# Making the MLP's inner activations in pieces, and moving the first copies at a pass's end, in a GLA and squared-ReLU layer

## The chip, the cores and the metric

One core of a Trainium2 chip. Time is that of the device for one execution of the whole kernel, in microseconds; the median of three runs of the kernel before is 1090.81 us (1090.51 to 1090.86). A profile is one further execution, taken by the hardware profiler.

Names used below: PE is TensorE (PEld its weight loads), DVE is VectorE, ACT is ScalarE, POOL is GpSimd, SP is the engine that issues the loads.

## The reference

One layer on 256 tokens of width 2048, all in float32: a normalization, a chunked gated linear attention with its projections, a residual sum, then the part that the change touches:

```python
h = h + _sq_relu_mlp(_rmsnorm(h, mlp_norm), w_up, w_down)   # w_up 2048 x 8192, w_down 8192 x 2048
def _sq_relu_mlp(h, w_up, w_down):
    a = jax.nn.relu(h @ w_up)
    return (a * a) @ w_down
```

and a final normalization. The inner activations are `a * a`, 8192 values for each token.

## The kernel before

**Products.** Each float32 operand is split into a high part (ACT, a cast, `copy_hi`, line 114) and a low part (DVE, the operand minus its high part, lines 124 and 147). A product is three matmuls: high by high, high by low, low by high. High and low parts of weights lie in five slots each (tags `hi` and `lo`), which are taken in turn, so a part can be made only when PE is through with the part five places back.

**Up.** The MLP runs in eight rounds of 1024 inner columns. A round has two groups of 512, and a group has eight up steps (`turned_steps`, line 182), each with one load of 512 KB, one high part, one low part and 24 matmuls. A group's sums lie in two PSUM banks.

**Forms.** When a group ends, DVE applies the ReLU and the normalization (`normalized`, line 714, output `su`), ACT squares (line 723, into `work`), DVE makes three or so differences (line 727) and ACT and DVE split all forms into high and low parts (`act`, lines 734 and 735). A group has two halves, and both use one buffer in `work` for their forms, one after the other.

**Down.** A pass is one round's activations by one column group of 512 outputs (`g`, four of them); the passes of a round go through the groups forward in odd rounds and backward in even ones, so the last group of a round is the first of the next. A pass has four units (`kp` 0 to 3), each of 256 inner rows: a load, high and low part of it, products. Most units are *summed* units: a Strassen scheme with seven products of blocks. They use sums of blocks of the weights, which DVE makes into `work` (line 830), and which are split into parts in their turn (`of_sums`, line 845; in the trace `hi<-work`, `lo<-work`). The first unit of a pass is mostly *plain*: full products and no sums. Where a pass has the same group as the one before it, its first unit is summed too.

**Banks.** A pass accumulates in four PSUM banks, P16, B32, P57 and BX4. At a pass's end to another group each bank is copied to SBUF (`settle`, which runs `copy_end`, line 750) and a free bank is loaded with the next group's state (`begin`, also line 750). Both are ACT copies of 128x512 elements. A copy out of a bank waits until PE is through with the bank.

**Order.** Up steps run 18 steps ahead of the units (`LEAD`). A unit issues its load, its parts and its products, then one up step goes in (`next(steps)` after the unit's `yield`), then the unit's `of_sums`. The order on each engine is made by a planner that goes by the program's order and its own costs; `issue_after(x)` puts what is issued in its block behind x on x's engine. `copy_hi` stays behind the last copy of a bank, and `copy_end` behind the last high part and the last copy, so their order on ACT is the program's. In the kernel before, forms are issued in one go, right behind the first up step of the next group, behind that step's low part on DVE. P16's settle and begin are issued in the unit before the first summed unit, behind its up step (line 854); P57's in the first summed unit ahead of `of_sums` (line 857); those of B32 and BX4 for the next pass in the pass's last unit ahead of `of_sums` (line 860).

Of the kernel before, what the change touches and what calls it, by code (L numbers as in the profile page):

```python
# [28 lines left out]
F32R = mybir.dt.float32r  # L29
# [3 lines left out]
P = 128  # L33
# [35 lines left out]
def tile_gla_mlp(ctx, tc, x, xt, cols, w_vg, w_in, w_gate, w_out, w_up, w_down, final_norm, out):  # L69
# [33 lines left out]
    def flush():  # L103
        while side:
            side.popleft()()
# [10 lines left out]
    def slots():  # L116
        return [wpool.tile([P, SLOT], F32R, tag=i, name=i) for i in ("hi", "lo")]
# [549 lines left out]
    def by_sums(m, g, kp):  # L667

        if m == ROUNDS - 1:
            return (g, kp) in ((0, 0), (0, 2), (1, 2))  # L670
        if m == ROUNDS - 2 and g == order_of(m)[-1]:
            return kp in (1, 2)
        return kp > 0 or m > 0 and g == order_of(m)[0]
# [9 lines left out]
    free = deque([*firsts, *aux_free, *others])  # L683

    def up():
        ended = []
        for m in range(ROUNDS):
            for q in range(MR // GT):
                taken = [free.popleft() for _ in range(2)]
                acc = [psum_bank(i, "up") for i in taken]  # L690
                even = (6,) if m == q == 0 else (0,) if m == 0 else (3,) if q == 0 else ()
                for _ in turned_steps(lambda kt: (hth[:, kt], htl[:, kt]), w_up, m * MR + q * GT, even, acc, 1):

                    while ended:
                        with tc.issue_after(last_lo[0].ins):
                            ended.pop(0)()
                    yield
                if m == 0:
                    flush()

                def end(m=m, q=q, acc=acc, taken=taken):
                    act = big.tile([P, 4 * G + 64], F32R, tag="BC"[q], name="act")[:, OFF:-16]
                    acts[m][q] = act = act.rearrange("p (b i f s) -> p b i f s", b=2, i=2, f=8)
                    normal = [normalized(b) for b in acc]
                    for b in range(2):
                        forms(m, 2 * q + b, normal[b], act[:, b])
                    free.extend(taken)

                ended.append(end)
        ended.pop()()  # L710

    def normalized(bank):
        s = tmp.tile([P, 2, T], F32, tag="t512", name="su", bufs=3)
        nc.vector.scalar_tensor_tensor(
            s, bank.rearrange("p (i t) -> p i t", i=2), 0.0, r2row.unsqueeze(1).to_broadcast([P, 2, T]),
            op0=ALU.max, op1=ALU.mult,
        )
        return s

    def forms(m, kp, s, act):  # L720
        ways = {by_sums(m, g, kp) for g in range(GROUPS)}
        f = work[:, 2].rearrange("p (f s) -> p f s", f=8)
        nc.scalar.activation(
            f[:, A12:].rearrange("p (t i) s -> p i t s", t=2), s.rearrange("p i (t s) -> p i t s", t=2), AF.Square
        )
        if True in ways:
            sub = lambda o, x, y: nc.vector.tensor_tensor(o, x, y, op=ALU.subtract)  # L727
            sub(f[:, S3 : S1 + 1], f[:, A21:].to_broadcast([P, 2, P]), f[:, A11 : A22 + 1])
            sub(f[:, S2], f[:, A11], f[:, S1])
            sub(f[:, S4], f[:, A12], f[:, S2])  # L730
        some = slice(0 if True in ways else A12, 8 if False in ways else A21)
        x = f[:, some].rearrange("p f s -> p (f s)")
        oh, ol = (act[:, i, some].rearrange("p f s -> p (f s)") for i in range(2))
        nc.scalar.copy(oh, x)
        nc.vector.tensor_tensor(ol, x, oh.bitcast(F32), op=ALU.subtract)  # L735
# [53 lines left out]
    def down(passes):  # L789

        ahead = pending = None
        units = 0
        for n, (m, g) in enumerate(passes):
            fresh = not n or passes[n - 1][1] != g
            if fresh:
                banks = ahead or {k: begin(k, g) for k in (B32, BX4)}
                if m == ROUNDS - 1:  # L800
                    flush()
            ends = n + 1 == len(passes) or passes[n + 1][1] != g
            first = min(kp for kp in range(KP) if by_sums(m, g, kp)) if fresh else None
            for kp in range(KP):
                last = ends and kp == KP - 1
                by_parts = by_sums(m, g, kp)

                def product(k, o, a, w, c, banks=banks, last=last):

                    bank = banks[k][1]  # L810
                    for i, (x, y) in enumerate(((0, 0), (0, 1), (1, 0))):
                        halves(bank[:, o], a[x], w[y][:, c], bank.name not in used, last and i == 2)
                        used.add(bank.name)

                raw = raw_tile()[:, : 2 * GT]
                c0 = m * MR + 2 * kp * P
                src = w_down[c0 : c0 + 2 * P, g * GT : (g + 1) * GT].rearrange("(i p) c -> p i c", p=P)
                last_load[0] = nc.sync.dma_start(out=raw.rearrange("p (i c) -> p i c", i=2), in_=src)
                w = parts(raw, 2 * GT, slots(), [(T * by_parts, 2 * GT)])
                at = lambda f, m=m, kp=kp: stationary(m, kp, f)  # L820
                block = lambda i: slice(i * T, (i + 1) * T)
                if by_parts:
                    product(P16, left, at(A11), w, block(1))
                    product(B32, right, at(A12), w, block(3))
                    product(B32, left, at(S4), w, block(2))
                    wk = work[:, n_sums[0] % 2]
                    n_sums[0] += 1
                    u = wk.rearrange("p (f s) -> p f s", f=4)
                    raw = raw.rearrange("p (f s) -> p f s", f=4)
                    add = lambda o, x, y: nc.vector.tensor_tensor(o, x, y, op=ALU.add)  # L830

                    with tc.issue_after(last_lo[0].ins):
                        add(u[:, :2], raw[:, :1].to_broadcast([P, 2, T]), raw[:, 1:3])
                        add(u[:, 2], u[:, 0], raw[:, 2])
                        last_sum[0] = add(u[:, 3], u[:, 2], raw[:, 3]).ins
                else:
                    for i in range(2):
                        for k, f in ((B32, (A11, A12)), (BX4, (A21, A22))):
                            product(k, slice(0, GT), at(f[i]), w, slice(i * GT, (i + 1) * GT))
                if pending:  # L840
                    pending()
                    pending = None
                yield

                def of_sums(wk=wk if by_parts else None, product=product, at=at):

                    with tc.issue_after(last_lo[0].ins):
                        wu = parts(wk, G, slots())
                    product(P57, left, at(S1), wu, block(0))
                    product(P57, right, at(S3), wu, block(1))  # L850
                    product(P16, right, at(S2), wu, block(2))
                    product(BX4, right, at(A22), wu, block(3))

                if fresh and kp == first - 1:
                    settle(P16)
                    banks[P16] = begin(P16, g)
                if fresh and kp == first:
                    settle(P57)
                    banks[P57] = begin(P57, g)
                if last:  # L860
                    if n + 1 < len(passes):
                        ahead = {k: begin(k, passes[n + 1][1]) for k in (B32, BX4)}
                    else:
                        last_banks(0)
                if by_parts:
                    if units + LEAD < UPS:
                        of_sums()
                    else:

                        pending = of_sums  # L870
                units += 1
                if fresh and kp == first:
                    settle(B32, BX4)
            if ends:

                def end(k, i, bank, g=g):
                    copy_end(home(k, g), two(bank))
                    free.append(i)

                late.update({k: lambda k=k, end=end, of=banks[k]: end(k, *of) for k in range(4)})  # L880
                begun.add(g)
                if m == ROUNDS - 1 or m == ROUNDS - 2 and g > 1:
                    late[BX4] = lambda f=late[BX4], g=g: (f(), side.extend(combine(g)))
# [147 lines left out]
```

## Time and profile before

| | |
|---|---|
| median of the runs | 1090.81 us |
| the profiled execution | 1090.18 us |
| its span, first to last instruction | 1088.1 us |
| PE busy | 1074.5 us |
| DVE busy | 830.7 us |
| ACT busy | 678.0 us |
| mean granted TensorE clock | 0.997 |
| loaded from HBM | 206.92 MB |

The MLP's matmuls run from about 381 us to the end; a round is about 87 us. In a group of instructions the line stands first, then the engine, the operation, output<-inputs, shape and count; behind the bar the time busy, the mean of one in ns, and the time in which its engine stood idle just before it, with what ended that. In a list of waits stand the total, the number and the longest wait. In order of time stand the start, the time and, in brackets, the idle time before. A window shows each engine's busy time with the number of its instructions, the granted clock, and the share and the rate of DMA.

### The profile page before, as it was taken

Reading aid. Unit: us, or ns where it says so; the run is one execution under the profiler, and the core shown is the slowest. Engines: PE = TensorE matmul, PEld = TensorE weight load, DVE = VectorE, ACT = ScalarE, POOL = GpSimd, SP = SyncE. Lnnn points to the kernel's source line nnn. Section 1 sums busy time; section 2 is a strip of 40 time slices with the busy share of each in tenths; the row PEclk is TensorE's granted clock in tenths of the full one; section 3 lists DMA queues with packets and bytes.
Section 4 is the critical chain, followed back from the end, with each engine's and each line's share of the span. In section 5 each row is a group of like instructions: output and inputs, shape, how many; then the busy total and the mean of one; then the engine's idle time right before and its main releaser. Section 6 shows DMA issues by size and latency. Waiting matters only on the chain.

```text
span 1088.1 us, 22191 instructions
## 1 busy us (share of the span) xinstructions
PE 1074.5 (99%) x9154; PEld 1069.0 (98%) x9154; DVE 830.7 (76%) x1140; ACT 678.0 (62%) x915; POOL 12.8 (1%) x39
## 2 busy tenths in 40 slices
PE   9999999999999999999999999999999999999996
PEld 9999999999999999999999999999999999999996
DVE  5777644656556466798898988988988989889976
ACT  6775445545545365576676677667667667667674
POOL 0000000100000000000000000000000000000000
PEclk9999999999999999999999999999999999999998
DMA  9957665555655656556555656565566565665562
GB/s 336 324 158 208 208 194 155 154 160 179 189 186 181 193 175 184 166 192 196 195 193 194 200 189 195 193 205 184 194 194 214 174 200 191 191 200 188 194 221 89
DMA packets 94788, 210.44 MB, mean 193 GB/s; under 512 B 6704, under 2 KB 7600, under 8 KB 94560
## 3 DMA queue, kind: packets, MB, share of 16 engines
q1 hardware_dynamic: 93728, 206.99, 59.4%
q10 hardware_dynamic: 960, 2.05, 0.5%
q8 instruction: 71, 1.16, 0.4%
q14 instruction: 29, 0.24, 0.1%
HBM read 206.92 MB, written 2.10 MB: 192 GB/s over the span
## 4 chain that ended last, share of the span: by engine, by line
PE 80%; DVE 12%; issue 3%; ACT 3%; DMA 2%; SPq 0%; ACTq 0%; POOLq 0%; POOL 0%; DVEq 0%
PE acc L158 44%; PE up L195 25%; PE acc L195 6%; DVE lo L124 5%; DVE work L830 3%; PE aux L195 2%; DVE lo L147 2%; ACT hi L114 2%; DMA raw<-in_w_vg 1%; PE aux L158 1%; PE aux L564 1%; DVE act L735 1%; DMA zz<-in_xt 1%; PE aux L492 1%; DVE work L727 1%
## 5 line engine op out<-in xcount | busy, mean ns | idle before, releaser
L114 ACT CAST hi<-raw 128x1024 fp32r<-128x1024 f32 (+3 forms) x386 | 370.6, 989 | 170.1 <-PE acc L158 109.5
L124 DVE TENSOR_TENSOR lo<-raw,hi 128x1024 fp32r<-128x1024 f32 (+3 forms) x226 | 247.6, 1097 | 170.6 <-ACT hi L114 170.0
L158 PE MATMUL acc<-hi,act 128*128 128x256 f32 x1832 | 341.5, 281 | 3.5 <-ACT hi L114 2.8
L158 PEld LDWEIGHTS acc<-hi,act 128*128 128x128 f32 x1832 | 280.5, 188 | 7.7 <-ACT hi L114 7.7
L195 PE MATMUL up<-hl,hi 128*128 128x256 f32 x1024 | 281.8, 279 | 0.0
L195 PE MATMUL up<-hh,hi 128*128 128x256 f32 x1024 | 281.1, 279 | 0.0
L195 PE MATMUL up<-hh,lo 128*128 128x256 f32 x1024 | 270.1, 279 | 0.0
L158 PE MATMUL acc<-lo,act 128*128 128x256 f32 x916 | 223.3, 280 | 0.5 <-DVE lo L124 0.4
L147 DVE TENSOR_TENSOR lo<-raw,hi 128x1024 fp32r<-128x1024 f32 x160 | 195.0, 1220 | 36.4 <-ACT hi L114 35.7
L195 PEld LDWEIGHTS up<-hh,hi 128*128 128x128 f32 x1024 | 192.5, 188 | 0.0
L195 PEld LDWEIGHTS up<-hl,hi 128*128 128x128 f32 x1024 | 192.5, 188 | 0.0
L195 PEld LDWEIGHTS up<-hh,lo 128*128 128x128 f32 x1024 | 185.7, 188 | 0.0
L114 ACT CAST hi<-work 128x1024 fp32r<-128x1024 f32 x92 | 96.8, 1053 | 116.2 <-DVE work L830 111.1
L158 PEld LDWEIGHTS acc<-lo,act 128*128 128x128 f32 x916 | 162.8, 188 | 1.3 <-DVE lo L124 1.1
L124 DVE TENSOR_TENSOR lo<-work,hi 128x1024 fp32r<-128x1024 f32 x92 | 112.4, 1222 | 4.8 <-ACT hi L114 2.8
L158 PE MATMUL acc<-hi,xA 128*128 128x256 f32 (+1 forms) x736 | 105.4, 281 | 0.0
L158 PEld LDWEIGHTS acc<-hi,xA 128*128 128x128 f32 x736 | 94.5, 190 | 0.2 <-ACT hi L114 0.2
L830 DVE TENSOR_TENSOR work<-work,raw 128x256 f32<-128x256 f32 x184 | 77.9, 424 | 4.2
L830 DVE TENSOR_TENSOR work<-raw 128x512 f32<-128x512 f32 x92 | 63.0, 685 | 0.0
L750 ACT COPY sums<-acc 128x512 f32<-128x512 f32 x46 | 26.7, 580 | 54.1 <-PE acc L158 54.1
L158 PE MATMUL acc<-lo,xA 128*128 128x256 f32 (+1 forms) x368 | 58.9, 280 | 0.1
L158 PEld LDWEIGHTS acc<-lo,xA 128*128 128x128 f32 x368 | 50.0, 189 | 0.3 <-DVE lo L124 0.3
(154 smaller groups left out, 1122.5 us busy)
## 6 DMA issues: line engine op xcount, KB each, us to landing
raw<-in_w_up SPq DMA_DIRECT2D x128, 512.0 KB, 4.6
raw<-in_w_down SPq DMA_DIRECT2D x128, 512.0 KB, 3.8
raw<-in_w_in SPq DMA_DIRECT2D x80, 512.0 KB, 3.7
raw<-in_w_out SPq DMA_DIRECT2D x32, 512.0 KB, 3.6
raw<-in_w_vg SPq DMA_DIRECT2D x14, 520.0 KB, 8.3
h<-in_x SPq DMA_DIRECT2D x4, 512.0 KB, 8.7
zz<-in_xt SPq DMA_DIRECT2D x3, 384.0 KB, 8.6
fb<-in_final_norm ACTq DMA_DIRECT2D x1, 1024.0 KB, 7.5
```

The source lines that it names most:

```text
L114: last_hi[0] = nc.scalar.copy(to, raw)
L124: last_lo[0] = nc.vector.tensor_tensor(lo[:, s], raw[:, s], hi[:, s].bitcast(F32), op=ALU.subtract)
L147: last_lo[0] = nc.vector.tensor_tensor(to[1], dst, to[0].bitcast(F32), op=ALU.subtract)
L158: nc.tensor.matmul(o[:, m], x, w[:, m], start=first and c == 0, stop=last, skip_group_check=True)
L195: nc.tensor.matmul(o, u[:, i, s], m, start=kt == 0 and n == 0 and j % 2 == 0, stop=kt == KT - 1 and n == 2, skip_group_check=True,)
L492: nc.tensor.matmul(o, kab[:, k[0], c0 + c, k[1] : k[1] + P], q(qt[:, c0 + c]), start=c == 0, stop=c == 1)
L564: nc.tensor.transpose(b[:, o + t * P : o + (t + 1) * P], src[:, t, kt * P : (kt + 1) * P], ident)
L727: sub = lambda o, x, y: nc.vector.tensor_tensor(o, x, y, op=ALU.subtract)
L735: nc.vector.tensor_tensor(ol, x, oh.bitcast(F32), op=ALU.subtract)
L750: last_end[0] = nc.scalar.copy(to, src).ins
L830: add = lambda o, x, y: nc.vector.tensor_tensor(o, x, y, op=ALU.add)
```

## The change

The forms of a group are made in four pieces after an empty one, one piece behind each of the next five up steps: nothing; the two `normalized` outputs (and the group's banks go free); square and differences of the first half; the split of the first half with square and differences of the second; the split of the second half. A piece is issued behind both the low part (on DVE) and the high part (on ACT) of its up step. After the last group the pieces go on in the units that have no up step any more.

P16's settle and begin move from the unit before the first summed unit to the first summed unit, behind the high and low part of its raw weights. The copies for the next pass's B32 and BX4, and at the last pass those of `last_banks`, move behind `of_sums` in the pass's last unit.

```diff
@@ -683,31 +683,42 @@
     free = deque([*firsts, *aux_free, *others])
 
     def up():
-        ended = []
+        ended = deque()
+
+        def piece():
+
+            if ended:
+                with tc.issue_after(last_lo[0].ins), tc.issue_after(last_hi[0].ins):
+                    ended.popleft()()
+
         for m in range(ROUNDS):
             for q in range(MR // GT):
                 taken = [free.popleft() for _ in range(2)]
                 acc = [psum_bank(i, "up") for i in taken]
                 even = (6,) if m == q == 0 else (0,) if m == 0 else (3,) if q == 0 else ()
                 for _ in turned_steps(lambda kt: (hth[:, kt], htl[:, kt]), w_up, m * MR + q * GT, even, acc, 1):
-
-                    while ended:
-                        with tc.issue_after(last_lo[0].ins):
-                            ended.pop(0)()
+                    piece()
                     yield
                 if m == 0:
                     flush()
-
-                def end(m=m, q=q, acc=acc, taken=taken):
-                    act = big.tile([P, 4 * G + 64], F32R, tag="BC"[q], name="act")[:, OFF:-16]
-                    acts[m][q] = act = act.rearrange("p (b i f s) -> p b i f s", b=2, i=2, f=8)
-                    normal = [normalized(b) for b in acc]
-                    for b in range(2):
-                        forms(m, 2 * q + b, normal[b], act[:, b])
-                    free.extend(taken)
-
-                ended.append(end)
-        ended.pop()()
+                ended.extend(ends(m, q, acc, taken))
+        while ended:
+            piece()
+            yield
+
+    def ends(m, q, acc, taken):
+
+        act = big.tile([P, 4 * G + 64], F32R, tag="BC"[q], name="act")[:, OFF:-16]
+        acts[m][q] = act = act.rearrange("p (b i f s) -> p b i f s", b=2, i=2, f=8)
+        normal = []
+
+        def start():
+            normal.extend(normalized(b) for b in acc)
+            free.extend(taken)
+
+        make = lambda b: forms(m, 2 * q + b, normal[b])
+        split = lambda b: form_parts(m, 2 * q + b, act[:, b])
+        return [nothing, start, lambda: make(0), lambda: (split(0), make(1)), lambda: split(1)]
 
     def normalized(bank):
         s = tmp.tile([P, 2, T], F32, tag="t512", name="su", bufs=3)
@@ -717,19 +728,24 @@
         )
         return s
 
-    def forms(m, kp, s, act):
-        ways = {by_sums(m, g, kp) for g in range(GROUPS)}
-        f = work[:, 2].rearrange("p (f s) -> p f s", f=8)
+    form = work[:, 2].rearrange("p (f s) -> p f s", f=8)
+    ways_of = lambda m, kp: {by_sums(m, g, kp) for g in range(GROUPS)}
+
+    def forms(m, kp, s):
+        f = form
         nc.scalar.activation(
             f[:, A12:].rearrange("p (t i) s -> p i t s", t=2), s.rearrange("p i (t s) -> p i t s", t=2), AF.Square
         )
-        if True in ways:
+        if True in ways_of(m, kp):
             sub = lambda o, x, y: nc.vector.tensor_tensor(o, x, y, op=ALU.subtract)
             sub(f[:, S3 : S1 + 1], f[:, A21:].to_broadcast([P, 2, P]), f[:, A11 : A22 + 1])
             sub(f[:, S2], f[:, A11], f[:, S1])
             sub(f[:, S4], f[:, A12], f[:, S2])
+
+    def form_parts(m, kp, act):
+        ways = ways_of(m, kp)
         some = slice(0 if True in ways else A12, 8 if False in ways else A21)
-        x = f[:, some].rearrange("p f s -> p (f s)")
+        x = form[:, some].rearrange("p f s -> p (f s)")
         oh, ol = (act[:, i, some].rearrange("p f s -> p (f s)") for i in range(2))
         nc.scalar.copy(oh, x)
         nc.vector.tensor_tensor(ol, x, oh.bitcast(F32), op=ALU.subtract)
@@ -817,6 +833,9 @@
                 src = w_down[c0 : c0 + 2 * P, g * GT : (g + 1) * GT].rearrange("(i p) c -> p i c", p=P)
                 last_load[0] = nc.sync.dma_start(out=raw.rearrange("p (i c) -> p i c", i=2), in_=src)
                 w = parts(raw, 2 * GT, slots(), [(T * by_parts, 2 * GT)])
+                if fresh and kp == first:
+                    settle(P16)
+                    banks[P16] = begin(P16, g)
                 at = lambda f, m=m, kp=kp: stationary(m, kp, f)
                 block = lambda i: slice(i * T, (i + 1) * T)
                 if by_parts:
@@ -851,24 +870,21 @@
                     product(P16, right, at(S2), wu, block(2))
                     product(BX4, right, at(A22), wu, block(3))
 
-                if fresh and kp == first - 1:
-                    settle(P16)
-                    banks[P16] = begin(P16, g)
                 if fresh and kp == first:
                     settle(P57)
                     banks[P57] = begin(P57, g)
+                if by_parts:
+                    if units + LEAD < UPS:
+                        of_sums()
+                    else:
+
+                        pending = of_sums
+                units += 1
                 if last:
                     if n + 1 < len(passes):
                         ahead = {k: begin(k, passes[n + 1][1]) for k in (B32, BX4)}
                     else:
                         last_banks(0)
-                if by_parts:
-                    if units + LEAD < UPS:
-                        of_sums()
-                    else:
-
-                        pending = of_sums
-                units += 1
                 if fresh and kp == first:
                     settle(B32, BX4)
             if ends:
```

More of the change, by code (lines that the diff above doesn't have):

```diff
@@ L859, in down @@
                     banks[P57] = begin(P57, g)
-                if last:
-                    if n + 1 < len(passes):
-                        ahead = {k: begin(k, passes[n + 1][1]) for k in (B32, BX4)}
-                    else:
-                        last_banks(0)
                 if by_parts:
@@ L871, in down @@
                 units += 1
+                if last:
+                    if n + 1 < len(passes):
+                        ahead = {k: begin(k, passes[n + 1][1]) for k in (B32, BX4)}
+                    else:
+                        last_banks(0)
                 if fresh and kp == first:
```

## The prediction

> **What bounds the kernel now.** I read the page first, then the waits of the matrix engine (PE), then its pace in windows, then VectorE (DVE) and ScalarE (ACT) in order of time at two places.
>
> ```profile
> span 1088.1 us, 22191 instructions
> PE 1074.5 (99%) x9154; PEld 1069.0 (98%) x9154; DVE 830.7 (76%) x1140; ACT 678.0 (62%) x915; POOL 12.8 (1%) x39
> ```
>
> PE is busy for 1074.5 of 1088.1 us, so a gain has to come from its idle 13.6 us or from the pace of its matmuls. The waits of its weight loads in the MLP, from 490 to 1030 us, and then in the last of the MLP, from 1030 to 1050 us:
>
> ```profile
> PEld acc L158 <- ACT hi L114: 6.3, 19, 0.6
> ```
>
> ```profile
> PEld acc L158 <- ACT hi L114: 1.4, 2, 1.1
> PEld acc L158 <- DVE lo L124: 1.1, 3, 0.4
> ```
>
> So 6.3 us in 19 waits, all for a high part, and 2.5 us at the end. Busy says nothing of the pace, so here are windows without a PE wait, with the count of matmuls in brackets (one is 0.28 us long and they start about 0.115 us apart, so each count holds some 2.4 that overlap an edge; I take these off):
>
> ```profile
> core 0: us, PE busy (x) PEld busy (x) DVE busy (x) ACT busy (x) POOL busy (x), PEclk, DMA share, GB/s
> 90.00:150.00 60.00, 60.00 (x532) 60.00 (x531) 38.37 (x59) 31.44 (x41) 2.33 (x16) 1.00 0.68 202
> 442.00:484.00 42.00, 42.00 (x373) 42.00 (x372) 34.38 (x48) 28.37 (x37) 0.00 (x0) 1.00 0.61 196
> 490.00:525.00 35.00, 35.00 (x300) 35.00 (x299) 31.53 (x44) 22.99 (x28) 0.00 (x0) 1.00 0.60 194
> 664.00:684.00 20.00, 20.00 (x179) 20.00 (x178) 16.30 (x22) 13.10 (x18) 0.00 (x0) 1.00 0.65 211
> 704.00:744.00 40.00, 40.00 (x342) 40.00 (x342) 33.76 (x47) 29.07 (x40) 0.00 (x0) 1.00 0.63 203
> 885.00:915.00 30.00, 30.00 (x257) 30.00 (x256) 24.59 (x36) 23.21 (x33) 0.00 (x0) 1.00 0.58 190
> ```
>
> There are two paces at one granted clock of 1.00: 60/529.6 = 113.3 ns and 42/370.6 = 113.3 ns in the first two rows, 35/297.6 = 117.6 ns in the third and 40/339.6 = 117.8 ns in the sixth. From 664 to 684 us it is fast again (20/176.6 = 113.2 ns), and a stall at 686 us stands between that row and the slow one behind it. The slow pace costs 1 - 113.3/117.7 = 3.7%.
>
> Why does PE wait? ACT and DVE around one change of passes without a stall, the two engines one after the other:
>
> ```profile
> 750.70 1.99 ACT L114 CAST hi<-raw 128x1024 fp32r<-128x1024 f32 x2
> 755.64 0.59 ACT L750 COPY sums<-acc 128x512 f32<-128x512 f32 x1 [2.95 <-PE acc L158]
> 756.26 0.59 ACT L750 COPY acc<-sums 128x512 f32<-128x512 f32 x1
> 756.78 1.78 ACT L114 CAST hi<-raw 128x768 fp32r<-128x768 f32 x2
> 759.07 0.59 ACT L750 COPY acc<-sums 128x512 f32<-128x512 f32 x1
> 760.22 1.06 ACT L114 CAST hi<-work 128x1024 fp32r<-128x1024 f32 x1 [0.55 <-DVE work L830]
> ...
> 753.11 1.22 DVE L147 TENSOR_TENSOR lo<-raw,hi 128x1024 fp32r<-128x1024 f32 x1
> 757.64 0.96 DVE L124 TENSOR_TENSOR lo<-raw,hi 128x768 fp32r<-128x768 f32 x1 [3.32 <-ACT hi L114]
> 758.52 0.69 DVE L830 TENSOR_TENSOR work<-raw 128x512 f32<-128x512 f32 x1
> 759.24 0.89 DVE L830 TENSOR_TENSOR work<-work,raw 128x256 f32<-128x256 f32 x2
> 761.30 1.23 DVE L124 TENSOR_TENSOR lo<-work,hi 128x1024 fp32r<-128x1024 f32 x1
> ```
>
> ACT has both high parts of the plain unit done at 752.7, then stands 2.95 us in front of the copy of P16's bank, which waits for PE to end the pass. The high part of the next unit's raw weights is behind that copy, so DVE stands 3.32 us. Whatever lead the two had over PE is set back here, and the whole page has 22 such waits:
>
> ```profile
> ACT sums L750 <- PE acc L158: 54.1, 22, 3.7
> ```
>
> After it, units follow in which DVE is nearly full. One round's window, and the groups of the forms:
>
> ```profile
> 663.60:750.20 86.60, 85.94 (x731) 85.14 (x730) 76.35 (x105) 59.75 (x78) 0.00 (x0) 1.00 0.60 195
> ```
>
> ```profile
> L735 DVE TENSOR_TENSOR act<-work,act 128x896 fp32r<-128x896 f32 (+2 forms) x32 | 34.8, 1086 | 0.6 <-ACT act L734 0.6
> L734 ACT CAST act<-work 128x896 fp32r<-128x896 f32 (+2 forms) x32 | 30.1, 941 | 10.7 <-DVE work L727 10.5
> L727 DVE TENSOR_TENSOR work<-work 128x128 f32<-128x128 f32 (+1 forms) x87 | 28.8, 331 | 0.2
> L714 DVE SCALAR_TENSOR_TENSOR su<-up,work 128x512 f32<-128x512 f32 x32 | 20.6, 683 | 0.0
> L723 ACT ACTIVATE work<-su 128x512 f32<-128x512 f32 x32 | 20.1, 629 | 11.6 <-DVE act L735 10.2 <-DVE su L714 1.4
> ```
>
> DVE is busy 76.35 of 86.6 us, and two groups of forms are in each round, each 2 x (0.68 + 3 x 0.33 + 1.09) = 5.5 us of DVE. Where the second group meets four summed units in a row, PE stalls:
>
> ```profile
> 684.87 1.05 ACT L114 CAST hi<-work 128x1024 fp32r<-128x1024 f32 x1 [2.90 <-DVE work L830]
> 689.73 0.63 ACT L723 ACTIVATE work<-su 128x512 f32<-128x512 f32 x1 [1.29 <-DVE act L735]
> 690.58 1.05 ACT L114 CAST hi<-work 128x1024 fp32r<-128x1024 f32 x1 [0.22 <-DVE work L830]
> 701.55 1.05 ACT L114 CAST hi<-work 128x1024 fp32r<-128x1024 f32 x1 [2.90 <-DVE work L830]
> ...
> 679.66 1.28 DVE L714 SCALAR_TENSOR_TENSOR su<-up,work 128x512 f32<-128x512 f32 x2
> 688.61 1.08 DVE L735 TENSOR_TENSOR act<-work,act 128x896 fp32r<-128x896 f32 x1
> 696.82 1.08 DVE L735 TENSOR_TENSOR act<-work,act 128x896 fp32r<-128x896 f32 x1
> ```
>
> The sums that ACT waits for at 684.87, 690.58 and 701.55 come out of DVE's queue behind these pieces, and PE waits for each of those three high parts. The lead is what is missing; DVE's total would do.
>
> **The change part by part.**
>
> *P16's copies behind one more high part.* At each change of passes to another column group, the high part of the first summed unit's raw weights goes ahead of P16's two copies. In the rows above it can start at 752.7 instead of 756.78. DVE is free at 753.11 + 1.22 = 754.33, subtracts until 755.3 and has the sums 1.5 us later, at 756.9. P16's copies stay at 755.64 to 756.85, since PE's end of the pass sets them. The up step's high part follows until 757.9, P57's copies until 759.1, and then the sums' high part, at 759.1 against 760.22. That is 1.1 us more lead; DVE's idle 3.32 us turns into two waits of about 1.1 us. PE wants P16 only at its next summed unit:
>
> ```profile
> 760.86 0.40 PE L158 MATMUL acc<-hi,act 128*128 128x256 f32 x2
> ```
>
> So the copies have 4.0 us of cover, which is what a late raw load could use up; behind the waiting copy on ACT stand every later high part and, through them, DVE and PE. If this cover went, one copy's 0.59 us would show at each of 21 changes, 12 us. I take a cost of nothing.
>
> *The next pass's two copies behind the sums' high part.* Two copies of 0.58 us, wanted a plain unit later; the plain unit's own high parts (1.99 us, row 750.70) are now behind them as they were before. Cost nothing; if the cover went, 1.2 us at each change.
>
> *The forms.* No instruction or DMA is added: 32 multiplications, 32 squares, 87 differences, 32 casts and 32 low parts stay, and SP's queue of loads keeps its order. They are issued as nothing, multiply (1.37 us of DVE), square and differences (1.0), low part and second differences (2.1), low part (1.1), one for each up step, and DVE and ACT both must have passed the step's parts first. Before, they started one unit earlier and the waits between ACT and DVE spread them over about 18 us (679.66 to 697.9), four units at 5.3 us. So the last piece lands in about the same place as before or a unit later, and the sum of the work is the same; what changes is that the multiplications leave the first unit free. By itself I count this at nothing, between a gain of 1.4 us a round (DVE's multiplications no longer in front of the sums at 684.87) and a loss of 1.7 us a group, which is the rival below. The first low part is due one unit after it is made; what would be late then is its 0.94 + 1.09 us on ACT and DVE.
>
> *The waits.* A round's stalls beside the 1.1 us of lead: with 6.3 us over six and a half rounds it is 1.0 us a round, the longest 0.6. The lead covers it, so the first term is -6.3 us; the other bound is 0, if the work that comes a unit later eats the lead.
>
> *The pace.* Fast stretches last while nothing disturbs PE (90 to 150, 442 to 484), and the one from 664 us ended at a stall; between 484 and 490 it turned slow without a wait that the list of waits shows, so a stall is not the only cause. Slow are about 480 of the 540 us from 490 to 1030. How it comes back to fast the rows don't show. Bounds: 0 and 480 x 3.7% = 17.8 us. I take a third, 5.9 us: with fewer stalls a fast stretch lasts, but it has to start, and at the fast pace DVE's spare 10.2 us a round shrinks to about 7 and the stalls partly return.
>
> The Trainium skill speaks against this term. Its page TensorE: Matmul & The Clock Gate, section Back-to-back issue gap, gives one gap for a matmul of N columns at the full clock, N/2.4 + 2.5 ns, an estimate of 109 ns here. By that rule there is no second pace to win, and the sum would be the waits alone; the trace has 113.3 and 117.7 ns at clock 1.00, so it doesn't agree.
>
> *The end.* The last forms and the summed units behind them hold DVE and ACT as before; 2.5 us of waits may go, or 1.3 us (a half's cast and low part of 512 elements, by the rows of 0.94 and 1.09 us no more than 2.0) may come. I take 0.
>
> **Sum.** The profiled execution took 1090.18 us, 2.1 more than its span: 1090.18 - 6.3 - 5.9 = 1078.0 us. It stands 0.63 us under the median of the runs, 1090.81, so the forecast is 1078.6 us; the times below are made from the median.
>
> **The rivals.**
>
> *All of it at the fast pace:* 1090.81 - 6.3 - 17.8 = 1066.7 us. For it: 42 us of MLP at 113.3 ns. Against: DVE's spare time is then least.
>
> *One pace, or the pace left as it lies:* the waits alone go, 1084.5 us. For it: the pace was slow in rows that hold no wait. Against: the change at 686 us.
>
> *The lead isn't gained:* the raw high part can't go earlier because its buffers aren't free, or the pieces a unit later take the lead up. The waits move and stay 6.3 us: 1090.8, 1089 to 1093. For it: DVE was without a gap from 677 to 703 us, and its total is the same.
>
> *Slower: the second square holds ACT.* In the unit of the low part and second differences ACT casts, then the square must wait for DVE's low part, since both use one buffer, and the sums' high part may be queued behind it.
>
> ```profile
> ACT work L723 <- DVE act L735: 10.2, 7, 2.4
> ```
>
> This is 1.09 + 0.63 = 1.7 us in front of what PE waits for, against 1.1 us of lead: 0.6 us in each of 14 groups, 8.4 us, with today's waits kept: 1099 us. It decides when a sums' high part starts over 1.1 us after its sums. Against: at 689.73 the square stood before the sums' high part and cost it 0.2 us.
>
> **How the numbers follow.** Chances: forecast 0.40 (its own range 1071 to 1084), all fast 0.17, one pace 0.17, lead not gained 0.14, slower 0.12. A difference under 0.2%, 2.2 us, can't be told from none here. The first three are faster, 0.74; the fourth is the same, 0.14; the last is slower, 0.12. The range 1065 to 1093 leaves out the slower case and nearly half of the all-fast one, 0.2 together.
>
> **What would show it.** The wait of the copies of sums for PE falls well below 54.1 us, and in its place a raw high part of 768 elements stands before that copy. DVE's 3.32 us is gone. The waits of weight loads from 490 to 1030 us fall from 6.3 us towards 0. Windows of 20 us between 490 and 1030 hold 179 matmuls more often than 172. It is wrong if the waits stay at 6 us, if a wait of PE for act shows up, or if the waits go and the counts stay.

## The result, and the profile after

The changed kernel takes 1064.80 us (median of four runs, 1063.72 to 1065.82) against 1090.66 us for the kernel before, timed beside it: a ratio of 0.9765, with a 95% interval of 0.9748 to 0.9782. That is 25.9 us, where 12.2 were forecast, 6.3 of waits and 5.9 of pace. The profiled execution is the slowest of the four, 1065.82 us.

The page of the changed kernel; the third line is the share of each engine in the chain that ended last:

```profile
span 1063.7 us, 22206 instructions
PE 1051.8 (99%) x9154; PEld 1050.4 (99%) x9154; DVE 831.6 (78%) x1140; ACT 681.9 (64%) x915; POOL 12.8 (1%) x39
...
PE 92%; DVE 3%; DMA 2%; issue 1%; ACT 1%; SPq 0%; POOLq 0%; POOL 0%; ACTq 0%; DVEq 0%
```

DVE and ACT have the work that they had (831.6 and 681.9 us against 830.7 and 678.0). PE has as many matmuls, 9154, and is busy 22.7 us less for them: most of the gain isn't idle time that went, it is pace. Windows of the changed kernel, the first five at the places of the prediction's table, the last over most of the MLP:

```profile
core 0: us, PE busy (x) PEld busy (x) DVE busy (x) ACT busy (x) POOL busy (x), PEclk, DMA share, GB/s
442.00:484.00 42.00, 42.00 (x373) 42.00 (x372) 36.31 (x50) 29.34 (x38) 0.00 (x0) 1.00 0.62 191
490.00:525.00 35.00, 35.00 (x310) 35.00 (x309) 32.24 (x46) 22.49 (x28) 0.00 (x0) 1.00 0.65 210
664.00:684.00 20.00, 20.00 (x179) 20.00 (x178) 18.60 (x28) 12.47 (x15) 0.00 (x0) 1.00 0.66 214
704.00:744.00 40.00, 40.00 (x355) 40.00 (x354) 36.23 (x49) 30.21 (x41) 0.00 (x0) 1.00 0.64 202
885.00:915.00 30.00, 30.00 (x267) 30.00 (x267) 26.55 (x37) 24.43 (x35) 0.00 (x0) 1.00 0.64 202
429.00:1010.00 581.00, 581.00 (x5124) 581.00 (x5123) 534.87 (x734) 415.00 (x530) 0.00 (x0) 1.00 0.63 201
```

The rows from 704 and from 885 us, which held 342 and 257 matmuls, hold 355 and 267. With the overhang of 2.4 taken off as in the prediction, the last row gives 581/5121.6 = 113.4 ns: the fast pace over nearly all of the MLP. PE is busy in all 581 us, and in this stretch its list of waits, which begins at 0.1 us, is empty; instruction by instruction no weight load stands as much as 20 ns. All that is left of its waits between 490 and 1030 us stands at the end, from 1010 to 1017 us:

```profile
PEld acc L158 <- DVE act L751: 1.8, 1, 1.8
PEld acc L158 <- ACT act L750: 0.9, 2, 0.7
PEld acc L158 <- DVE lo L124: 0.2, 1, 0.2
```

The lead around one change of passes, in order of time on ACT, on DVE, and then PE's first product of the first summed unit:

```profile
698.58 2.73 ACT L114 CAST hi<-raw 128x1024 fp32r<-128x1024 f32 x3
701.60 0.59 ACT L766 COPY sums<-acc 128x512 f32<-128x512 f32 x1 [0.29 <-PE acc L158]
702.22 0.59 ACT L766 COPY acc<-sums 128x512 f32<-128x512 f32 x1
702.75 1.05 ACT L114 CAST hi<-raw 128x1024 fp32r<-128x1024 f32 x1
...
704.84 1.05 ACT L114 CAST hi<-work 128x1024 fp32r<-128x1024 f32 x1
...
701.93 0.95 DVE L124 TENSOR_TENSOR lo<-raw,hi 128x768 fp32r<-128x768 f32 x1
...
707.07 0.28 PE L158 MATMUL acc<-hi,act 128*128 128x256 f32 x1
```

The 768-element high part is now the last of the three casts in front of the copy of P16's bank, and ACT waits 0.29 us for PE there instead of 2.95; DVE follows at 701.93 instead of standing 3.32 us. The sums' high part starts 707.07 - 704.84 = 2.23 us ahead of PE, against 760.86 - 760.22 = 0.64 us in the rows of before. The copies' wait for PE over the whole execution (54.1 us before):

```profile
ACT sums L766 <- PE acc L158: 22.0, 23, 2.9
```

**Where the 25 us lie.** The last matmul of an up step starts at 1025.7 us before and at 1000.6 after: 25.1 us. Of these 6.3 are the waits and 17.8 the 480 us of slow stretches at 3.7%; 1.0 I don't assign. From there to the end the two kernels take 62.4 and 63.1 us, so the tail gained nothing.

Two theories came out of this. *Pace follows waits:* PE has two paces in this kernel, a wait puts it on the slow one, and the moved copies and the pieces gain by leaving no wait at all. *Pace follows position:* where the parts of the weights lie sets the pace, and the new order of slots or the shifted steps happen to fall well. A shifted step is one that `turned_steps` is given in `even`: the second half of its parts lies 16 floats further on in its slot. The first round has two, each later one has one.

### The profile page after: what moved, and what is told of

It reads as the page before. It is cut to its first block, busy times and chain, and to the rows that moved or that the text cites. A ratio compares the mean times of both kernels' runs of the same rounds, so it can differ in the third digit from the quotient of the medians.

```text
span 1063.7 us, 22206 instructions
## 1 busy us (share of the span) xinstructions
PE 1051.8 (99%) x9154; PEld 1050.4 (99%) x9154; DVE 831.6 (78%) x1140; ACT 681.9 (64%) x915; POOL 12.8 (1%) x39
## 3 DMA queue, kind: packets, MB, share of 16 engines
q10 hardware_dynamic: 960, 2.05, 0.5%
## 4 chain that ended last, share of the span: by engine, by line
PE 92%; DVE 3%; DMA 2%; issue 1%; ACT 1%; SPq 0%; POOLq 0%; POOL 0%; ACTq 0%; DVEq 0%
PE acc L158 50%; PE up L195 31%; PE acc L195 6%; PE aux L195 2%; DVE lo L124 1%; DMA raw<-in_w_vg 1%; PE aux L158 1%; DVE work L849 1%; PE aux L564 1%; ACT hi L114 1%; DMA zz<-in_xt 1%; PE aux L492 1%; DVE lo L147 0%; SPq L150 0%; ACT h L766 0%
## 5 line engine op out<-in xcount | busy, mean ns | idle before, releaser
L114 ACT CAST hi<-raw 128x1024 fp32r<-128x1024 f32 (+3 forms) x386 | 375.0, 990 | 185.3 <-PE acc L158 111.8
L158 PE MATMUL acc<-hi,act 128*128 128x256 f32 x1832 | 329.7, 277 | 2.1 <-DVE act L751 1.6
L158 PEld LDWEIGHTS acc<-hi,act 128*128 128x128 f32 x1832 | 277.7, 188 | 2.7 <-DVE act L751 1.8
L195 PE MATMUL acc<-xA,hi 128*128 128x256 f32 x288 | 49.2, 276 | 0.0
```

Source lines behind the costliest of these rows:

```text
L114: last_hi[0] = nc.scalar.copy(to, raw)
L158: nc.tensor.matmul(o[:, m], x, w[:, m], start=first and c == 0, stop=last, skip_group_check=True)
L195: nc.tensor.matmul(o, u[:, i, s], m, start=kt == 0 and n == 0 and j % 2 == 0, stop=kt == KT - 1 and n == 2, skip_group_check=True,)
```

## The experiments

### One half of the change at a time

The pieces alone, with all copies where they were:

```diff
-                if fresh and kp == first:
-                    settle(P16)
-                    banks[P16] = begin(P16, g)
...
+                if fresh and kp == first - 1:
+                    settle(P16)
+                    banks[P16] = begin(P16, g)
                 if fresh and kp == first:
                     settle(P57)
...
+                if last:
+                    ...
                 if by_parts:
```

> The forms in pieces alone, the copies at a pass's end as in the kernel before. Theory 1 (lead): the lead over PE comes from the high part that goes ahead of P16's copies, and the stalls go because of it; then this run keeps most of the waits for high parts (4 to 8 us from 490 to 1010 us), stays mostly at the slow pace, and takes 1083 to 1093 us. Theory 2 (burst): the forms in one go are what empties the lead; then this run has under 1 us of waits, the fast pace, and takes 1064 to 1068 us.

Measured: 1089.96 us, a ratio of 0.9997 (0.9988 to 1.0006). PE's waits in the MLP (490 to 1010 us, 6.3 us in 19 before), the copies' wait in the whole, and windows at the places above:

```profile
PEld acc L158 <- ACT hi L114: 3.4, 10, 0.6
...
ACT sums L766 <- PE acc L158: 53.0, 23, 3.7
```

```profile
490.00:520.00 30.00, 30.00 (x267) 30.00 (x267) 27.23 (x35) 18.10 (x22) 0.00 (x0) 1.00 0.62 205
...
885.00:915.00 30.00, 30.00 (x256) 29.97 (x256) 26.52 (x37) 22.83 (x32) 0.00 (x0) 1.00 0.59 192
```

The pieces take half of the waits away, 2.9 us (what is left, 3.4 us, is a little under the 4 to 8 of the first theory), and the time doesn't move by what can be told. One stretch that was slow is fast (267 in 30 us from 490), the later ones are slow as before, the two that were fast (660 to 685 and 833 to 859 us) are slow now, and the end costs more (63.3 us behind the last up step against 62.4).

The copies alone, forms in one go as before; and of these the move of P16 alone:

```diff
                 w = parts(raw, 2 * GT, slots(), [(T * by_parts, 2 * GT)])
+                if fresh and kp == first:
+                    settle(P16)
+                    banks[P16] = begin(P16, g)
...
-                if fresh and kp == first - 1:
-                    settle(P16)
-                    banks[P16] = begin(P16, g)
```

To the first of the two belongs as well that `if last:` with `begin` and `last_banks` goes behind `of_sums`.

> The copies moved alone (P16's and those of the next pass), the forms in one go as before. Theory 1 (lead): under 1.5 us of waits from 490 to 1010 us and mostly the fast pace, 1065 to 1073 us. Theory 2 (burst): waits near 6 us, the slow pace, 1085 to 1093 us. If neither part does it alone, both this run and the one with pieces alone stay above 1078 us.

> P16's copies moved alone; the next pass's two copies and the forms as before. If only P16's place matters, within 2 us of the run with both copies moved. If the next pass's copies matter (they stand in front of the sums' high part, 1.2 us at each of some 20 changes), 3 us or more above that run.

Measured: both moves 1072.02 us, 0.9837 (0.9822 to 0.9851); P16 alone 1074.56 us, 0.9863 (0.9847 to 0.9880). With P16 alone, from 425 to 1010 us:

```profile
PEld acc L158 <- ACT hi L114: 0.7, 2, 0.3
...
ACT sums L750 <- PE acc L158: 48.6, 21, 3.2
```

So P16's copies are the larger part of the change, though the copies' wait hardly falls. ACT still stands in front of the copy out of P16's bank, but all three casts of raw weights are now ahead of that copy, where there were two:

```profile
742.83 2.73 ACT L114 CAST hi<-raw 128x1024 fp32r<-128x1024 f32 x3
748.77 0.59 ACT L750 COPY sums<-acc 128x512 f32<-128x512 f32 x1 [3.21 <-PE acc L158]
```

The two waits of PE that are left, at 610 and 865 us, stand at no such copy. With both moves, in the same stretch:

```profile
ACT sums L750 <- PE acc L158: 26.0, 21, 2.9
```

The wait falls by 22.6 us, which is about the time of the two copies of 0.55 us at each of 21 changes: they now run where ACT stood. The two kernels are 2.5 us apart, between the two forecasts (within 2 us, or 3 or more). Windows with both moves:

```profile
620.00:655.00 35.00, 35.00 (x311) 35.00 (x310) 32.72 (x47) 26.41 (x36) 0.00 (x0) 1.00 0.64 210
704.00:744.00 40.00, 40.00 (x342) 40.00 (x342) 35.86 (x49) 29.99 (x40) 0.00 (x0) 1.00 0.62 202
790.00:850.00 60.00, 60.00 (x532) 60.00 (x531) 54.52 (x75) 44.05 (x60) 0.00 (x0) 1.00 0.61 199
885.00:915.00 30.00, 30.00 (x257) 30.00 (x256) 27.17 (x37) 22.16 (x30) 0.00 (x0) 1.00 0.62 197
```

This kernel has no wait in its list from 425 to 1010 us, and yet two slow stretches. Instruction by instruction, three weight loads stand 46 to 49 ns behind their high part, at 610.4, 693.2 and 861.8 us. At 610.4 the pace stays fast. At 693.2 it turns slow for 83 us, until the shifted step at 776.6; at 861.8 for 162 us, past the next shifted step, until a wait of 69 ns at 1023.4. The two stretches cost 245 us x 3.7% = 9.1 us. The pieces, worth nothing alone, take these three waits out, and 1072.02 becomes 1064.80.

### One stall put into the fast kernel, and the shifted steps taken out

If pace follows waits, one stall in the changed kernel must cost much more than itself, and without shifted steps there should be nothing to bring the pace back. In the first kernel ten copies of ACT are added ahead of one sums' high part; in the second the shifted steps from the second round on are taken out; the third has both edits:

```diff
                 def of_sums(wk=wk if by_parts else None, product=product, at=at):
 
+                    if units == 50:
+                        idle = tmp.tile([P, 512], F32, tag="t512", name="idle", bufs=3)
+                        for _ in range(10):
+                            copy_end(idle, h[:, 0, G : G + 512])
```

```diff
-                even = (6,) if m == q == 0 else (0,) if m == 0 else (3,) if q == 0 else ()
+                even = (6,) if m == q == 0 else (0,) if m == 0 else ()
```

> The changed kernel with ten more ACT copies of 512 elements (5.8 us) ahead of one sums' high part, in the third unit of the fourth round, at about 695 us. They make PE wait once. Theory 1: PE waits 1 to 5 us there, its matmuls start 117 to 118 ns apart from then on until the next shifted step, some 80 us later, and 113.4 ns apart again behind it; the time is 1064.8 plus the wait plus 3 us, 1069 to 1073. Rival (the slow pace is a matter of the slots or of ACT's and DVE's load): the pace stays at 113.4 ns on both sides of the wait, and the time is 1064.8 plus the wait alone.

> The changed kernel with the step whose second tile lies 16 floats further (the fourth up step of a round) laid out as the other steps, from the second round on. Theory 1: the fast pace lasts until a wait of PE, and the shifted step only brings it back after one; with no wait before 1010 us the pace stays fast and the time is within 1.5 us of 1064.8. Rival: the shifted step is needed in each round, or the fast pace ends by itself after some 80 us; then the matmuls turn slow after 525 us and the time is 1078 us or more.

> The same one wait, and no shifted step from the second round on. Theory 1: slow from the wait to the end of the MLP, some 300 us at 3.7%, 11 us: the time is 8 us above that of the run with the wait and the shifted steps, 1077 to 1081. Rival: it comes back to 113.4 ns by itself within 100 us, and the two runs are within 3 us.

Measured, one stall: 1074.98 us in one execution, 10.2 above the changed kernel's median and 9.2 above its profiled execution. Its waits from 690 to 705 us, and windows on both sides:

```profile
PEld acc L158 <- ACT hi L114: 2.3, 3, 1.0
PEld acc L158 <- DVE lo L124: 0.3, 1, 0.3
```

```profile
650.00:685.00 35.00, 35.00 (x311) 35.00 (x311) 32.67 (x46) 24.56 (x32) 0.00 (x0) 1.00 0.66 211
705.00:740.00 35.00, 35.00 (x300) 35.00 (x299) 31.28 (x45) 26.54 (x36) 0.00 (x0) 1.00 0.63 206
820.00:855.00 35.00, 35.00 (x300) 35.00 (x299) 31.99 (x44) 23.68 (x30) 0.00 (x0) 1.00 0.57 188
885.00:915.00 30.00, 30.00 (x267) 30.00 (x267) 27.25 (x38) 22.50 (x31) 0.00 (x0) 1.00 0.61 193
```

35/308.6 = 113.4 ns ahead of the stall, 35/297.6 = 117.6 ns behind it. The stall is 2.6 us; the slow stretch is 167.5 us long, 6.2 us of time; together they make 8.8 of the 9.2. The load of DVE and ACT doesn't explain the pace: the changed kernel is fast from 704 to 744 us with 36.23 and 30.21 us of work in 40, and this one is slow from 705 us with 31.28 and 26.54 in 35, about the same shares. I had expected the next shifted step to end it. The one near 775 us did not, the one near 864 did, so the price is higher than expected.

Without shifted steps and without the stall: 1064.48 us, 0.9763 (0.9747 to 0.9779), no change, and fast from 408 to 945 us without one wait. There it turns slow, again without a wait, and stays so to the waits at the end, some 69 us or 2.6 us of time. I had expected it to stay fast. Rows of both paces:

```profile
490.00:525.00 35.00, 35.00 (x312) 35.00 (x311) 32.23 (x46) 22.48 (x28) 0.00 (x0) 1.00 0.63 207
...
885.00:915.00 30.00, 30.00 (x267) 30.00 (x267) 26.58 (x37) 24.06 (x33) 0.00 (x0) 1.00 0.65 208
...
950.00:985.00 35.00, 35.00 (x299) 35.00 (x299) 33.30 (x49) 26.01 (x35) 0.00 (x0) 1.00 0.64 209
```

The stall without shifted steps: 1079.20 us in one execution, slow to the waits at the end, some 330 us on:

```profile
650.00:685.00 35.00, 35.00 (x311) 35.00 (x311) 32.67 (x44) 24.56 (x31) 0.00 (x0) 1.00 0.65 210
705.00:740.00 35.00, 35.00 (x299) 35.00 (x298) 31.28 (x44) 26.23 (x35) 0.00 (x0) 1.00 0.63 207
885.00:915.00 30.00, 30.00 (x257) 30.00 (x256) 27.10 (x38) 21.79 (x30) 0.00 (x0) 1.00 0.57 181
960.00:1000.00 40.00, 40.00 (x342) 40.00 (x341) 37.71 (x55) 29.12 (x40) 0.00 (x0) 1.00 0.59 194
```

330 x 3.7% = 12.2 us; the partner without the stall pays 2.6 of these too, in its own slow 69 us. With 2.7 us of stall and 1.6 us of half clock at the end, which the partner doesn't have (priced in the next section), that makes 13.9; the two profiled executions stand 1079.20 - 1064.49 = 14.7 apart. It is 4.2 us above the kernel with the stall and the shifted steps, where I had expected 8, since one of those steps didn't act. So here a wait set the slow pace, the pace held after the wait was over, and a shifted step could end it. Pace by position alone falls: the 705 row has the parts in the same places with and without the stall, and another pace.

But *pace follows waits* is too narrow as well. In the kernel before, the fast row from 664 us of the prediction began at a wait, of 0.2 us at 659.5 us:

```profile
PEld acc L158 <- ACT hi L114: 0.2, 1, 0.2
```

```profile
646.00:659.00 13.00, 13.00 (x113) 13.00 (x112) 10.87 (x17) 9.62 (x14) 0.00 (x0) 1.00 0.54 176
660.00:685.00 25.00, 25.00 (x223) 25.00 (x223) 21.23 (x30) 16.17 (x23) 0.00 (x0) 1.00 0.63 208
```

That is 13/110.6 = 117.5 ns ahead of it and 25/220.6 = 113.3 ns behind it; the fast stretch from 833 us began at such a wait too. So waits stand where the pace turns either way, and it turns without one as well (at 945 us in the kernel without shifted steps, between 484 and 490 us in the kernel before). That a wait can bring the slow pace is shown by the edit; what brings the fast one, beside some shifted steps, is not.

The same edit in the kernel before, without the shifted steps from the second round on:

> The kernel before without shifted steps from the second round on. Theory 1: its waits keep it slow, and the few fast stretches that began at a shifted step go; the two of 25 us at 660 and 833 us began at a wait and may stay. 1090 to 1093 us. Rival: if the shifted steps had been of use to the kernel before, 1094 us or more.

Measured: 1090.20 us, 0.9996 (0.9987 to 1.0006). From 490 to 1010 us:

```profile
PEld acc L158 <- ACT hi L114: 5.9, 19, 0.6
```

With 19 waits in the way, fast stretches that the shifted steps start are soon over, 2 to 3 us behind the steps at 611, 698 and 871 us in the kernel before; here they are worth nothing that can be told. Without them the stretch from 833 us is still fast, behind a wait of 0.2 us.

### The end

In the changed kernel the last group's forms begin one step later, behind the empty piece, and PE waits for them. Without the empty piece for the last group:

```diff
-        return [nothing, start, lambda: make(0), lambda: (split(0), make(1)), lambda: split(1)]
+        wait = [nothing] if (m, q) != (ROUNDS - 1, 1) else []
+        return [*wait, start, lambda: make(0), lambda: (split(0), make(1)), lambda: split(1)]
```

> The changed kernel, with the empty piece left out for the last group alone. The changed kernel waits 2.9 us for act at 1010 to 1016 us and its matmuls then start 213 ns apart for 3.4 us. If the wait comes from the pieces being late by their place, it falls by 1 us or more and the time falls 2 to 4 us under the changed kernel's 1064.8; if DVE's work there is the limit, the wait keeps its size and the time stays within 1 us of 1064.8.

Measured: 1063.37 us (1063.31 to 1063.63), 0.9757 (0.9743 to 0.9772). Its PE waits from 1008 to 1022 us:

```profile
PEld acc L158 <- DVE lo L124: 1.8, 3, 0.8
PEld acc L158 <- ACT hi L114: 0.3, 1, 0.3
```

No wait for `act` is left, and 2.1 us of waits stand where 2.9 stood. The profiled executions differ by more, 1065.82 - 1063.38 = 2.4 us. The other part is a stretch at half clock that the changed kernel's profiled execution has behind its waits and this one's doesn't. Windows of the changed kernel at that place, and some rows of PE:

```profile
1012.00:1016.00 4.00, 2.05 (x13) 1.43 (x11) 3.56 (x5) 1.56 (x3) 0.00 (x0) 1.00 0.42 119
1016.20:1019.40 3.20, 3.20 (x15) 3.20 (x16) 2.18 (x3) 3.20 (x5) 0.00 (x0) 0.50 0.60 197
```

```profile
1016.16 0.79 PE L158 MATMUL acc<-hi,act 128*128 128x256 f32 x2 [0.46 <-ACT act L750]
...
1018.03 1.48 PE L158 MATMUL acc<-hi,act 128*128 128x256 f32 x6
```

15 matmuls in 3.2 us at a granted clock of 0.50. The stretch is 3.4 us long with matmuls 213 ns apart, so it costs 3.4 x (1 - 113.4/213) = 1.6 us; with 0.8 us of waits that makes the 2.4. The kernel with this edit is the fastest so far by its median, 1.4 us below the changed kernel, which lies between the two forecasts, and the two spreads don't meet; but 1.4 us is 0.13%, and the ratios' intervals overlap.

Two more edits on top of this one. The tail runs at the slow pace, near 118 ns, so two of its tiles are laid 16 floats further on; in another kernel unit `kp` 2 of the first column group of the last round is plain instead of summed:

```diff
-                w = parts(raw, 2 * GT, slots(), [(T * by_parts, 2 * GT)])
+                to = slots()
+                if (m, g, kp) == (ROUNDS - 1, 1, 1):
+                    to = [a[:, WRAP : WRAP + 2 * GT] for a in to]
+                w = parts(raw, 2 * GT, to, [(T * by_parts, 2 * GT)])
...
+        if kt == 1:
+            into = [a[:, WRAP : WRAP + G] for a in into]
```

```diff
-            return (g, kp) in ((0, 0), (0, 2), (1, 2))
+            return (g, kp) in ((0, 0), (1, 2))
```

> The kernel whose last group starts one step earlier, with two tiles of down weights behind its last waits put 16 floats further in their slots, so that weight loads and moving operand stand to each other as in the shifted up step. If it is this relation that brings the fast pace back, the matmuls behind the second of these tiles (from about 1025 to 1058 us) start 113.4 ns apart instead of 117.7, and the time falls 1 to 1.5 us under 1063.4, which would show at both or one of the two tiles only if each works about half the time. If it is something else in the up step, the pace stays 117.7 and the time within 0.5 us of 1063.4.

> The kernel whose last group starts one step earlier, with one of the last summed units (last round, first group, third unit) made plain: three matmuls more on PE (0.35 us), and on DVE three sums and one low part less (about 2.7 us). If DVE's load sets the 2.2 us of waits from 1010 to 1020 us, they fall by 1 us or more and the time is 1062 to 1063. If ACT's and DVE's order sets them, the time stays at 1063.4 or rises by the 0.35 us.

Measured: 1064.12 us, 0.9757 (0.9741 to 0.9773), and 1063.15 us, 0.9748 (0.9734 to 0.9763); neither can be told from the kernel that they start from. With the shifted tiles the pace behind 1017 us stays at 117.8 ns. With the plain unit, the waits from 1008 to 1030 us:

```profile
PEld acc L158 <- ACT hi L114: 2.2, 3, 1.2
PEld acc L158 <- DVE lo L124: 0.2, 1, 0.2
```

The waits at 1010 to 1020 us fall to 0.7 us, and one of 1.2 and one of 0.4 us come at 1026 instead: the stall moved.

## Why the prediction was wrong

**The pace** is the term that failed: "I take a third, 5.9 us" of 17.8. All of it came, 12 us more than the forecast has, and the time is that of the rival "All of it at the fast pace", 1066.7, less 1.9 us. Both reasons for the third were wrong. "It has to start": the changed kernel is fast from 408 us on but for some 2 us in each shifted step, and nothing in its middle makes it slow. "The stalls partly return": they didn't, with DVE busy 534.87 of 581 us, 92%. I had the stall at 686 us in front of a slow stretch and took it for one cause among several; the experiment with one stall shows the size of it, 6.2 us of pace for 2.6 us of wait, and 12.2 without shifted steps. How much of the 17.8 would come couldn't be worked out from the rows: which waits turn the pace, and which way, isn't known even now. What turned the kernel before slow between 484 and 490 us stays open: no weight load there stands as much as 20 ns.

**The waits**, -6.3 us, were right, and so was the mechanism: "The lead covers it." P16's move alone leaves 0.7 us of them. The lead that I sized at 1.1 us is 2.23 - 0.64 = 1.6 at the changes shown.

**P16's copies** at no cost: right; nothing behind them was late. Alone they are worth 1.4% of the time.

**The next pass's two copies**, "Cost nothing": mis-sized. They bring 1074.56 - 1072.02 = 2.5 us beside P16's move. With P16 alone two weight loads wait 0.7 us together, where with both moves they stand 46 and 49 ns, and some 39 us more are slow (1.4 us); why those two waits are shorter isn't shown.

**The forms**, "By itself I count this at nothing": right for the pieces alone, 0.9997. It was wrong to add the parts up, since on top of the moved copies the pieces are worth 7.2 us: the last 46 to 49 ns waits go, and with them two slow stretches.

**The end**, taken at 0 between -2.5 and +2.0 us: the sum came out near it (62.4 and 63.1 us), but not for the reason given: the 2.5 us of waits went, and 2.9 us of others and 1.6 us of half clock came. That would be 2.0 us more, and 0.7 were measured; the rest I don't assign. A wait of PE for `act`, which I had named as a sign that the forecast is wrong, did show, 2.7 us of it. It means that the forms are late in the one place where no further up step follows; it says nothing on the other 580 us.

**The rivals.** "One pace" falls: both paces stand in the rows on the two sides of one stall, 308.6 and 297.6 matmuls in 35 us at clock 1.00. The Trainium skill's page TensorE: Matmul & The Clock Gate, section Back-to-back issue gap, states N/2.4 + 2.5 ns as "the *isolated* single-MM gap" and says that in a stream of weight loads and matmuls, as here, both set the spacing; for that it has about 81 ns at 128 columns and 131 ns at 512, and nothing at 256. So the prediction's 109 ns was not the page's figure for such a stream, and the section has nothing on a second pace; the trace's 113.4 and 117.6 ns lie between its two figures. "The lead isn't gained" and the square that holds ACT did not come: no wait of PE from 425 to 1010 us.

## What to carry to other kernels

Where matmuls of one shape and one granted clock come at two paces, count matmuls in windows, look for the last wait ahead of each slow stretch, and price it with that stretch: here 48 and 49 ns of wait were followed by 83 and 162 us at 3.7%. Removing half of the waits brought nothing here and removing all but two nearly 16 us, so two edits that each leave some waits are to be tried together. A copy that waits for the end of a pass goes behind every high part that could run without it.

## What the runs showed of the hardware that I had not expected

**A pace with a memory.** At granted clock 1.00, weight load and matmul pairs of 128x256 come every 113.4 or every 117.7 ns. A stall of 2.6 us switched from the first to the second, and waits of 48 and 49 ns stood where it switched too; one of 46 ns, at 610.4 us, did not switch it. Waits of 0.2 us at 659.5 and 833 us of the kernel before stood where it switched back, and at 945 us of the kernel without shifted steps it turned slow with no wait. The slow pace lasted 83, 162, 167.5 and some 330 us, the last with no shifted step in the way. Of the steps that lie 16 floats further on, some brought the fast pace back and some did not, and in the tail two such tiles changed nothing. Why is open: what differs between the steps, and between the waits, wasn't found.

**Half clock after short waits.** In the changed kernel PE was busy 2.05 us from 1012 to 1016 us, 1.34 of the 3.41 us up to 1016.15, and then had a granted clock of 0.50 for 3.4 us. Three other kernels here have such a stretch: the pieces alone, and the two with the stall. PE was busy 1.37, 1.32 and 1.77 us in the 3.41 us ahead of it. With 1.1 and 0.7 us of waits at the same place (the kernel without shifted steps) PE was still busy 2.05 us in the 3.41 us from 1013.10, and the clock stayed at 1.00. The Trainium skill's page TensorE: Matmul & The Clock Gate, section What's actually happening, gives windows of about 3.4 us, an idle one of which halves the clock; the length agrees with the 3.4 us here, but no window of that length without work stands ahead of it in these traces: one in which PE was busy for 1.77 us was enough.
